# Queries of both layers and of the index: the split into two parts on whole tiles, the placing over partition halves by SBUF transfers

## The chip, the cores and the metric

The kernel runs on one core of a Trainium2 chip. The metric is the device time of one execution in microseconds (us), the median of several runs. Five engines matter: PE (TensorE, the matrix products), DVE (VectorE), ACT (ScalarE), POOL (GpSimd) and SP (SyncE, which here only issues transfers). Each engine runs its own instructions strictly in order, and waits for others by semaphores.

## The reference, cut to what matters

The model has two layers over 512 tokens of width 1024, in float32, with a squared-ReLU MLP behind each attention. What the change touches are three sets of queries:

```python
# layer A: sparse attention
q, k, v, qi, ki, wi = split(xn @ w_in)           # 16 query heads, 4 key heads, 8 index heads of 64
qi, ki = rope(qi), rope(ki)                      # index queries (8 heads) and index key (1 head)
score  = sum_h wi[t,h] * relu(qi[t,h] . ki[s])   # for blocks of 128 queries
sel    = top 128 of score among the allowed keys
o      = softmax(rope(q) . rope(k) / 8, over sel) @ v
# layer B: forgetting attention
q = xn @ w_q                                     # 16 heads of 64
o = softmax(q . k / 8 + decay, causal) @ v
```

## The kernel before, in words

**Precision.** A float32 factor is kept as two parts, hi (rounded to the fast matmul format) and lo (the rest), and a product is made of three: hi*hi, hi*lo, lo*hi. `split(hi, lo, src)` makes both: one ACT instruction writes hi, one DVE instruction writes lo = src*scale - hi.

**Two parts in one contraction.** A head has 64 features, half of the 128 partitions. The kernel uses the free half: a query tile has hi of one head on partitions 0 to 63 and lo of the same head on 64 to 127, and for the next head the halves the other way round, so that with the key's parts stacked likewise two matmuls of 128 rows do the work of three products. `unpair(dst, b, scale)` makes such a tile from a PSUM bank `b`, whose upper 64 partitions hold one head and whose lower 64 the other. In the names below `up` is partitions 0 to 63 and `dn` 64 to 127. In the kernel before it takes four instructions of 64 partitions: two on ACT for the two hi halves and two on DVE for the two lo halves. Those of lo read one half of the partitions and write the other.

**Who calls it.** `stacks` transposes a roped tile on PE (`qT<-ident,qr`, four 128x128) and calls `unpair`. `idx1` does so for the index queries `qst` of the query tiles t = 1, 2, 3 (tile 0 needs no selection), three calls; `qdone` for layer A's queries `qs`, four tiles and two halves of the heads, eight calls; `qstack` calls `unpair` directly for layer B's queries `qo`, eight calls: 19 in all.

**Who reads them.** `scores(t)` multiplies `qst` with the index key `kid` (`ix<-kid,qst`, 16 matmuls per tile); ACT takes the ReLU of each (`rl<-ix`), and DVE sums them with weights into `mask` (seven `mask<-rl,wi,mask` per tile, then one MEMSET for the keys that are not allowed). `topk(t)` then runs 16 rounds of MAX and MATCH_REPLACE over `mask` on DVE. The logits `lg<-kd,qs` and `lg<-kdup,qo` read the other two.

**Stages of layer A, by the trace.** Projections of the index (`tp<-whi,xT` and `tp<-wlo,xT` of 264 and 320 columns) to about 40 us, then keys, values and queries (512 columns), the selection and the softmax to about 188 us, the output projection after that. Layer B's queries are made at 580 to 612 us.

**What sets the order.** All instructions are first recorded and then ordered by a planner (`schedule`), which has a cost for each instruction, a latency between engines and a fixed landing time for transfers; it fills the wait of one chain with ready instructions of others. The order it finds is fixed when the program is built, and each engine runs its list. Every instruction of the program is written by the recorder's `emit`, so that all rows of the profile show its line, L423; rows are told apart by the tile names.

**Queues.** SP issues all plain transfers, in one order: weights (`raw<-in_w_...`), the inputs x and h, the output. POOL issues the transfers that add while they write (`wlo<-raw`: `wlo` holds -hi, and raw is added to it). ACT also makes the hi parts of weights (`whi<-raw`).

Of the kernel before, what the change touches and what calls it, by code (L numbers as in the profile page):

```python
# [125 lines left out]
class Recorder:  # L126
# [299 lines left out]


CFG = {
# [10 lines left out]
def body(ctx, tc, a, out):  # L439
    nc = tc.nc  # L440
    rec = Recorder(nc)
    V, S, G, PE, SP = (rec.engine(e) for e in ("DVE", "ACT", "POOL", "PE", "SP"))
# [35 lines left out]
    def scr(shape, name, dt=F32):  # L478
        return rec.tile(p_s2, shape, dt, name)

    def bank(shape, name):
        return rec.tile(p_ps, shape, F32, name, quotas.get(name))

    def small(n, name):
        return rec.tile(p_sm[n], [128, n], F32, name)
# [13 lines left out]
    def split(hi, lo, src, scale=None):  # L499
        if scale is None:  # L500
            S.copy(hi, src)
            V.tensor_tensor(lo, src, f32(hi), op=OP.subtract)
        else:
            S.activation(hi, src, AF.Copy, scale=scale)
            V.scalar_tensor_tensor(lo, src, scale, f32(hi), op0=OP.mult, op1=OP.subtract)
# [569 lines left out]
    def mlp(xT, xf, wu, wd, after, last=False):  # L1075
# [83 lines left out]
        for ci in range(4):  # L1159
# [34 lines left out]
            lastc = ci == 3  # L1194
# [2 lines left out]
                o = h[i][:, 512 * half + c.start:512 * half + c.stop]  # L1197
                add(o, src[:, c], o)

            far = CFG["dlast" if last and lastc else "dfar"]  # L1200

            def wop(y, n):
                return wop_(y, n in far)
# [88 lines left out]

    ys = {}
    mlp(xT, xf, a["w_up"][0], a["w_down"][0], afterA)

    qo = [big([128, 2, T], "qo") for _ in range(8)]
# [73 lines left out]
    e = scr([16, T], "e")  # L1370
# [62 lines left out]
    def attn(p, ks, bts):  # L1433
        pts = {}
        for e in range(2):
            q = qo[p][:, e, :]
            b0, b1, b2 = [bank([128, T], "pT") for _ in range(3)]
            rcs = small(4, "rc") if CFG["rcb"] else None
            sts = small(4, "st") if CFG["rcb"] else None
            ls = {}  # L1440
            l01 = scr([128, 384], "l")
            for t in CFG["bord"]:
                n = 128 * (t + 1)
                b = bank([128, 512], "lg")
                for i in range(2):
                    PE.matmul(b[:, :n], q[:, 128 * t:128 * t + 128], ks[e][:, i, :n], start=i == 0, stop=i == 1)
                l, mn = scr([128, n], "l") if t > 1 else l01[:, 128 * t:128 * t + n], small(1, "mn")
                st = sts[:, t:t + 1] if CFG["rcb"] else small(1, "st")
                V.tensor_tensor_reduce(out=l, in0=b[:, :n], in1=bts[e][t], op0=OP.add, op1=OP.min,
                                       scale=-1.0, scalar=BIG, accum_out=mn)  # L1450
                S.activation(l, l, AF.Exp, bias=mn, scale=-1.0, accum_out=st)
                ls[t] = l, st
            if CFG["rcb"]:
                V.reciprocal(rcs, sts)
            for t in CFG["bord"]:
                l, st = ls[t]
                if CFG["rcb"]:
                    rc = rcs[:, t:t + 1]
                else:
                    rc = small(1, "rc")  # L1460
                    V.reciprocal(rc, st)
                if CFG["bsc"] == "V":
                    V.tensor_scalar(l, l, rc, None, op0=OP.mult)
                else:
                    G.tensor_scalar(l, l, rc, 0.0, op0=OP.mult, op1=OP.add)
                PE.transpose(b0[:, 128 * t:128 * t + 128], l[:, 0:128], ident)
                if t >= 1:
                    PE.transpose(b1[:, 128 * t - 128:128 * t], l[:, 128:256], ident)
                if t >= 2:
                    PE.transpose(b2[:, 128 * t - 128:128 * t], l[:, 256:384], ident)  # L1470
                if t == 3:
                    PE.transpose(b2[:, 0:128], l[:, 384:512], ident)

            pts[e] = []
            for b in (b0, b1[:, 0:384], b2[:, 0:384]):
                if p in CFG["pvb"]:
                    pts[e].append(scr(b.shape, "pf"))
                    S.copy(pts[e][-1], b)
                else:
                    pts[e].append((scr(b.shape, "ph", F32R), scr(b.shape, "pl", F32R)))  # L1480
                    split(pts[e][-1][0], pts[e][-1][1], b)
        parts = ((0, slice(0, T), 0), (1, slice(128, T), 1), (2, slice(384, T), 3), (2, slice(256, T), 2))
        rng = lambda j: slice(0, 128) if j == 3 else slice(128, 384) if j == 2 else slice(0, T - 128 * j)
        if p in CFG["pvb"]:

            o = bank([128, T], "pv")
            for e in (1, 0):
                for x, c, j in parts:
                    PE.matmul(o[:, c] if e else o[0:64, c], vbf[j, p] if e else vbf[j, p][:, 0:64],
                              pts[e][x][:, rng(j)], start=j == 0, stop=j == 2)  # L1490
        else:
            o = oB[p // 2][:, p % 2, :] if oB else scr([128, T], "o")
            for e in range(2):

                pv, u = bank([128, T], "pv"), scr([64, T], "u")
                for x, c, j in parts:
                    for i in range(2):
                        PE.matmul(pv[:, c], vb[j][p // 4][:, (2 * p + e) % 8].flat(), pts[e][x][i][:, rng(j)],
                                  start=j + i == 0, stop=j == 2 and i == 1)
                S.copy(u, pv[64:128])  # L1500
                V.tensor_tensor(o[64 * e:64 * e + 64], pv[0:64], u, op=OP.add)
        if not oB:
            split(qo[p][:, 0, :], qo[p][:, 1, :], o)
        elif p in CFG["pvb"]:
            S.copy(oB[p // 2][:, p % 2, :], o)
# [4 lines left out]
    for p in range(8):  # L1510
        if p < 7:
            kss[p + 1] = kproj(p + 1)
        attn(p, kss[p], bts[p])
        if p < 7:
            bts[p + 1] = bias(p + 1)
# [18 lines left out]
    def afterB(t):  # L1534
# [15 lines left out]
        SP.dma_start(out[128 * t:128 * t + 128, early], hg[0])  # L1550

    mlp(xT, xf, a["w_up"][1], a["w_down"][1], afterB, last=True)

    order = rec.schedule()
# [33 lines left out]
```

## Time and profile before

| what | value |
|---|---|
| median of 3 runs | 1151.32 us (1151.09 to 1151.34) |
| profiled execution | 1147.72 us |
| its span on the core | 1145.9 us, granted clock 0.998 |
| PE busy | 1124.8 us, 98% of the span |
| DVE busy | 942.1 us, 82% |
| ACT busy | 802.5 us, 70% |
| POOL busy | 226.6 us, 20% |

The span is from the first to the last instruction; 1.8 us of the execution's time lie around it. Busy shares are means over stages with different limits, so the rows below go by stretches of time. A row that says `x16` stands for 16 instructions, with its busy time and the mean of one.

### The profile page before, as it was taken

What the parts mean: (1) busy time and instruction counts of PE and PEld (TensorE: products, weight loads), DVE (VectorE), ACT (ScalarE), POOL (GpSimd) and SP (SyncE); (2) the same over time, 40 slices, a digit from 0 to 9 for tenths busy, and PEclk for the clock granted to TensorE, in tenths of its full rate; (3) what the DMA queues carried; (4) which work ended last, traced back from release to release, by engine and by line L of the source; (5) the groups of instructions that cost most, each with busy time, mean ns of one, the idle gap of its engine ahead of it and who ended that gap; (6) DMA issues with size and microseconds to landing.
All of it is one profiled execution on the core that took longest, in us unless ns stands there. A gap on an engine that the chain in (4) does not pass through costs nothing.

```text
span 1145.9 us, 18603 instructions
## 1 busy us (share of the span) xinstructions
PE 1124.8 (98%) x6695; PEld 980.5 (86%) x6695; DVE 942.1 (82%) x1667; ACT 802.5 (70%) x1402; POOL 226.6 (20%) x378
## 2 busy tenths in 40 slices
PE   8999999999999999999999999999999999999997
PEld 8877778899899898898887878788898998998986
DVE  7999997488979979979856369764789989899687
ACT  8942899677667667569783268997676765666693
POOL 0212455100000100101110087862000100101130
PEclk9999999999999999999999999999999999999999
DMA  9871262836674674895975313597355756747892
GB/s 334 182 166 37 79 180 46 193 97 183 181 200 138 169 206 134 184 277 147 240 165 111 112 50 106 158 239 177 82 182 150 188 163 182 198 153 201 227 218 89
DMA packets 116364, 186.95 MB, mean 163 GB/s; under 512 B 8072, under 2 KB 63392, under 8 KB 116272
## 3 DMA queue, kind: packets, MB, share of 16 engines
q1 hardware_dynamic: 101008, 130.18, 34.5%
q0 software_dynamic: 15264, 55.58, 26.3%
q8 instruction: 53, 0.87, 0.3%
q14 instruction: 39, 0.32, 0.1%
HBM read 125.94 MB, written 4.23 MB: 114 GB/s over the span
## 4 chain that ended last, share of the span: by engine, by line
PE 77%; DVE 8%; issue 6%; ACT 6%; DMA 2%; POOL 1%; DVEq 0%; POOLq 0%; ACTq 0%
PE tp L423 38%; PE up L423 22%; PE qp L423 4%; PE pv L423 3%; PE lg L423 3%; PE pT L423 3%; PE kp L423 2%; DMA ulo<-raw 2%; ACT l L423 1%; DVE mask L423 1%; PE yT L423 1%; ACT whi L423 1%; ACT xT L423 1%; DVE h L423 1%; ACT kdup L423 1%
## 5 line engine op out<-in xcount | busy, mean ns | idle before, releaser
L423 PE MATMUL tp<-dhi,xhi 128*128 128x512 f32 (+1 forms) x452 | 172.1, 389 | 1.7 <-DVE h L423 1.0
L423 PE MATMUL tp<-dlo,xhi 128*128 128x512 f32 (+1 forms) x452 | 171.9, 388 | 0.0
L423 PE MATMUL tp<-dhi,xlo 128*128 128x512 f32 (+1 forms) x452 | 170.9, 388 | 0.0
L423 ACT CAST dhi<-raw 128x1024 fp32r<-128x1024 f32 x112 | 114.9, 1046 | 66.6 <-DVE raw L423 51.4
L423 PE MATMUL up<-t,uhi 128*128 128x256 f32 x896 | 148.9, 284 | 1.6 <-DVE r L423 1.6
L423 POOL DMA_DIRECT2D ulo<-raw x42 | 36.5, 870 | 516.6 <-ACT ulo L423 420.8
L423 DVE TENSOR_TENSOR dlo<-raw,dhi 128x1024 fp32r<-128x1024 f32 x100 | 121.3, 1224 | 14.9 <-ACT dhi L423 9.3
L423 PEld LDWEIGHTS up<-t,uhi 128*128 128x128 f32 x896 | 126.7, 192 | 3.3 <-DVE r L423 2.6
L423 PE MATMUL tp<-whi,xT 128*128 128x512 f32 (+2 forms) x432 | 127.6, 373 | 0.6 <-ACT xT L423 0.5
L423 PE MATMUL up<-xT,uhi 128*128 128x256 f32 x672 | 117.2, 285 | 0.2 <-DVE r L423 0.2
L423 DVE TENSOR_TENSOR raw<-raw 128x1024 f32<-128x1024 f32 x92 | 111.3, 1223 | 0.3
L423 PEld LDWEIGHTS tp<-dhi,xhi 128*128 128x128 f32 x452 | 84.9, 188 | 20.4 <-ACT xhi L423 1.1
L423 PEld LDWEIGHTS up<-xT,uhi 128*128 128x128 f32 x672 | 99.1, 191 | 2.8 <-DVE r L423 1.8
L423 PEld LDWEIGHTS tp<-dhi,xlo 128*128 128x128 f32 x452 | 84.7, 188 | 17.1
L423 PEld LDWEIGHTS tp<-dlo,xhi 128*128 128x128 f32 x452 | 84.9, 188 | 16.6
L423 PE MATMUL up<-t,ulo 128*128 128x256 f32 x448 | 96.1, 283 | 0.0
L423 PEld LDWEIGHTS tp<-whi,xT 128*128 128x128 f32 x432 | 78.2, 188 | 13.3 <-ACT xT L423 0.7
L423 ACT CAST uhi<-raw 128x1024 fp32r<-128x1024 f32 x84 | 86.0, 1044 | 4.8 <-PE up L423 4.7
L423 DVE TENSOR_TENSOR h<-tp,h 128x512 f32<-128x512 f32 (+1 forms) x97 | 65.7, 688 | 23.2 <-PE tp L423 23.1
L423 POOL TENSOR_SCALAR l<-l,rc 128x128 f32<-128x128 f32 (+3 forms) x128 | 69.6, 560 | 59.6 <-DVE rc L423 43.0
L423 PE MATMUL up<-xT,ulo 128*128 128x256 f32 x336 | 80.7, 283 | 0.0
L423 POOL DMA_DIRECT2D wlo<-raw x52 | 45.8, 902 | 176.2 <-ACT wlo L423 82.6
(213 smaller groups left out, 2717.6 us busy)
## 6 DMA issues: line engine op xcount, KB each, us to landing
raw<-in_w_down_dram SPq DMA_DIRECT2D x96, 512.0 KB, 5.3
raw<-in_w_up_dram SPq DMA_DIRECT2D x64, 512.0 KB, 5.6
wlo<-raw POOLq DMA_DIRECT2D x52, 512.0 KB, 7.1
ulo<-raw POOLq DMA_DIRECT2D x42, 512.0 KB, 5.5
raw<-in_w_kv_b_dram SPq DMA_DIRECT2D x16, 512.0 KB, 7.8
raw<-in_w_in_a_dram SPq DMA_DIRECT2D x12, 512.0 KB, 8.4
dlo<-raw POOLq DMA_DIRECT2D x12, 512.0 KB, 6.2
raw<-in_w_o_a_dram SPq DMA_DIRECT2D x8, 512.0 KB, 5.6
```

The lines of the kernel that those rows point to most:

```text
L423: getattr(self.engs[o.eng], o.fn)(*a, **k)
```

## The change

One setting changes, `CFG["swap"]` from False to True. With it, `unpair` no longer writes the halves from PSUM. It splits the whole bank, all 128 partitions at once, into two scratch tiles `nh` (hi) and `nl` (lo), with one ACT and one DVE instruction, and then has SP issue four transfers from SBUF to SBUF, of 64 partitions x 2 KB each, that place the halves:

```python
hi, lo = scr([128, 512], "nh", F32R), scr([128, 512], "nl", F32R)
split(hi, lo, b, scale=scale)
SP.dma_start(f32(d)[up, 0], f32(hi)[up])
SP.dma_start(f32(d)[dn, 0], f32(lo)[up])
SP.dma_start(f32(d)[dn, 1], f32(hi)[dn])
SP.dma_start(f32(d)[up, 1], f32(lo)[dn])
```

The diff, cut to its lines (the two new settings `dend` and `bsv` are empty, and change nothing):

```diff
 CFG = {
-    "land": 4.0, "pw": 700, "p7": (), "swap": False, "dup": False, "ufar": ("1", "2", "4"), "dfar": (), "dlast": ("1", "2", "5", "6", "3", "7"),
+    "land": 4.0, "pw": 700, "p7": (), "swap": True, "dup": False, "ufar": ("1", "2", "4"), "dfar": (), "dend": (), "bsv": (), "dlast": ("1", "2", "5", "6", "3", "7"),
...
-            far = CFG["dlast" if last and lastc else "dfar"]
+            far = CFG["dlast" if last and lastc else "dend" if lastc else "dfar"]
...
-                if CFG["bsc"] == "V":
+                if CFG["bsc"] == "V" or (p, e) in CFG["bsv"]:
```

The planner sees other instructions and finds another order. It differs in layer A's attention (up to about 235 us of the trace) and around layer B's queries; elsewhere only tile numbers differ. Three places follow, with tile names as above; a name after `<-` is what is read, and `x4` stands for four in a row.

**SP, layer A**: the loads behind the last weights of the input projection. Before:

```order
L423 DMA raw<-in_w_in_a_dram 128x2x512 x8
L423 DMA raw<-in_w_o_a_dram 128x2x512 x8
L423 DMA g<-in_g_mlp_dram 128x1024
L423 DMA raw<-in_w_up_dram 128x8x128 x4
L423 DMA h<-in_x_dram 128x1024 x4
```

and now, from the placing of the sixth `qs` on (the three of `qst` and the first five of `qs`, four transfers each, stand ahead of these rows, behind the eight loads of `w_in_a`):

```order
L423 DMA qs<-nh 64x512 x2
L423 DMA qs<-nl 64x512 x2
L423 DMA raw<-in_w_o_a_dram 128x2x512 x4
L423 DMA qs<-nh 64x512 x2
L423 DMA qs<-nl 64x512 x2
L423 DMA raw<-in_w_o_a_dram 128x2x512 x4
L423 DMA raw<-in_w_up_dram 128x8x128 x4
L423 DMA g<-in_g_mlp_dram 128x1024
L423 DMA qs<-nh 64x512 x2
L423 DMA qs<-nl 64x512 x2
L423 DMA h<-in_x_dram 128x1024 x4
```

The loads of `w_o_a` now stand behind the sixth and seventh placing of `qs`, those of `h` behind the eighth. Earlier on the same queue, three of the four `w_in_a` loads of 320 columns have moved ahead of the last two loads of x.

**PE, layer A**: the first index scores `ix` of tile 1. Before, from the last projection products ahead of them:

```order
L423 MATMUL tp<-whi,xT 128x320 x2
L423 MATMUL tp<-wlo,xT 128x320
L423 MATMUL tp<-whi,xT 128x320 x2
L423 MATMUL tp<-wlo,xT 128x320
L423 MATMUL tp<-whi,xT 128x320 x2
L423 MATMUL tp<-wlo,xT 128x320
L423 MATMUL ix<-kid,qst 128x256 x16
L423 MATMUL qT<-ident,qr 128x128 x3
L423 MATMUL tp<-whi,xT 128x320 x2
L423 MATMUL tp<-wlo,xT 128x320
```

and now:

```order
L423 MATMUL tp<-whi,xT 128x320
L423 MATMUL qT<-ident,qr 128x128
L423 MATMUL tp<-whi,xT 128x512 x6
L423 MATMUL tp<-wlo,xT 128x512
L423 MATMUL tp<-whi,xT 128x512
L423 MATMUL qT<-ident,qr 128x128 x3
L423 MATMUL tp<-whi,xT 128x512
L423 MATMUL tp<-wlo,xT 128x512
L423 MATMUL tp<-whi,xT 128x512
L423 MATMUL tp<-wlo,xT 128x512
L423 MATMUL ix<-kid,qst 128x256 x2
L423 MATMUL tp<-whi,xT 128x512 x2
```

The 16 `ix` of tile 1 stood in one piece, behind 59 products of 320 columns, 5 `qT` and none of 512 columns. Now the first stand behind 72 products of 320 columns, 12 `qT` and 12 of 512 columns, and the 16 are spread, with 20 more of 512 columns between them.

**DVE, layer A**: the lo parts of `qst` and the weighted sum of tile 1 (`mask<-rl,wi,mask` 128x256, closed by the MEMSET). Before:

```order
L423 TENSOR_TENSOR rtmp<-tp,rot 128x5x32
L423 TENSOR_TENSOR qr<-tp,rot 128x320
L423 SCALAR_TENSOR_TENSOR qst<-qT,qst 64x512 x2
L423 TENSOR_TENSOR rtmp<-tp,rot 128x5x32
L423 TENSOR_TENSOR qr<-qr,rtmp 128x320
L423 SCALAR_TENSOR_TENSOR mask<-rl,wi,mask 128x256 x6
L423 SCALAR_TENSOR_TENSOR qst<-qT,qst 64x512
L423 SCALAR_TENSOR_TENSOR mask<-rl,wi,mask 128x256
L423 SCALAR_TENSOR_TENSOR qst<-qT,qst 64x512
L423 MEMSET mask 64x64
L423 TENSOR_TENSOR rtmp<-tp,rot 128x5x32
L423 TENSOR_TENSOR qr<-tp,rot 128x320
```

and now:

```order
L423 SCALAR_TENSOR_TENSOR nl<-qT,nh 128x512
L423 TENSOR_TENSOR rtmp<-tp,rot 128x5x32
L423 TENSOR_TENSOR qr<-tp,rot 128x320
L423 TENSOR_TENSOR rtmp<-tp,rot 128x5x32
L423 TENSOR_TENSOR qr<-qr,rtmp 128x320
L423 SCALAR_TENSOR_TENSOR nl<-qT,nh 128x512
L423 SCALAR_TENSOR_TENSOR mask<-rl,wi,mask 128x256 x7
L423 MEMSET mask 64x64
L423 MAX mx<-mask 128x8
L423 MATCH_REPLACE mask<-mx,mask 128x256
L423 MAX mx<-mask 128x8
L423 MATCH_REPLACE mask<-mx,mask 128x256
```

Four half-tile `qst` stood ahead of the MEMSET, now three whole `nl`, of all three tiles (the third further up); the rope of the last tile (`rtmp`, `qr`, `rtmp`, `qr` of 320 columns) stood behind the MEMSET and now stands ahead of it.

## Rows read from the trace of the kernel before

**Rows 1.** The page's first part: busy time of each engine in us, share of the span, number of instructions.

```profile
PE 1124.8 (98%) x6695; PEld 980.5 (86%) x6695; DVE 942.1 (82%) x1667; ACT 802.5 (70%) x1402; POOL 226.6 (20%) x378
```

**Rows 2.** Busy time by stretches: layer A's attention from 42 us, its second part, the time just before it, the time after it, and a piece of its middle. Columns: start and end of the stretch, its length, then busy us and number of instructions of PE, PEld, DVE, ACT and POOL, the granted TensorE clock as a share, the busy share of the 16 DMA engines, GB/s.

```profile
42.00:188.00 146.00, 143.89 (x738) 112.84 (x738) 140.72 (x418) 102.41 (x246) 48.33 (x77) 1.00 0.43 106
110.00:188.00 78.00, 77.66 (x433) 60.08 (x432) 73.49 (x238) 70.18 (x189) 35.86 (x65) 1.00 0.38 102
30.00:42.00 12.00, 11.56 (x79) 10.79 (x78) 9.88 (x27) 11.90 (x22) 2.64 (x4) 1.00 1.06 248
188.00:235.00 47.00, 46.73 (x232) 38.20 (x231) 24.35 (x57) 35.32 (x66) 11.64 (x15) 1.00 0.63 135
90.00:120.00 30.00, 29.03 (x147) 22.49 (x146) 29.62 (x93) 10.53 (x35) 7.28 (x11) 1.00 0.11 36
```

**Rows 3.** The same for the stretch in which layer B's queries are made.

```profile
600.00:620.00 20.00, 20.00 (x90) 15.44 (x89) 10.25 (x13) 10.79 (x14) 2.62 (x3) 1.00 0.74 162
```

**Rows 4.** Two of DVE's groups by operation and shape: line, engine, operation, out<-in, shapes, number | busy us, mean ns of one | idle time ahead of them.

```profile
L423 DVE TENSOR_TENSOR pl<-pT,ph 128x512 fp32r<-128x512 f32 x42 | 27.3, 685 | 6.2 <-ACT ph L423 6.1
L423 DVE SCALAR_TENSOR_TENSOR qs<-qT,qs 64x512 fp32r<-64x512 f32 x16 | 11.0, 688 | 0.4
```

**Rows 5.** The same of ACT.

```profile
L423 ACT CAST ph<-pT 128x512 fp32r<-128x512 f32 x42 | 23.0, 593 | 0.7 <-PE pT L423 0.4
L423 ACT ACTIVATE qs<-qT 64x512 fp32r<-64x512 f32 x16 | 9.5, 592 | 27.8 <-PE qT L423 27.6
```

**Rows 6.** Instructions that write and read the tiles `qo` and `qs`: number, duration in ns (least, median, most), first and last start in us.

```profile
L423 PEld LDWEIGHTS lg<-kdup,qo x128: 186/188/208, 667.1 to 772.6; 128*128 128x128 f32 x128
L423 DVE SCALAR_TENSOR_TENSOR qo<-qp,qo x16: 683/688/694, 580.8 to 610.8; 64x512 fp32r<-64x512 f32 x16
L423 PEld LDWEIGHTS lg<-kd,qs x128: 186/189/215, 109.3 to 186.8; 128*128 128x128 f32 x128
L423 DVE SCALAR_TENSOR_TENSOR qs<-qT,qs x16: 683/688/694, 83.9 to 154.8; 64x512 fp32r<-64x512 f32 x16
```

**Rows 7.** Transfers by kind: number, KB each, median us from issue to landing; the last row is the tile view of the output tile, with the time in ns that SP takes to issue one.

```profile
raw<-in_w_in_a_dram SPq DMA_DIRECT2D x12, 512.0 KB, 8.4
raw<-in_w_o_a_dram SPq DMA_DIRECT2D x8, 512.0 KB, 5.6
h<-in_x_dram SPq DMA_DIRECT2D x4, 512.0 KB, 9.8
out_dram<-hg SPq DMA_DIRECT2D x8, 256.0 KB, 2.7
cd<-cum SPq DMA_DIRECT2D x1, 32.0 KB, 1.6
L423 SPq DMA_DIRECT2D out_dram<-hg x8: 332/382/402, 1131.3 to 1142.7; - x8
```

**Rows 8.** SP's queue in time: start, length, and the transfers issued in it.

```profile
17.55 7.76 SPq L423 DMA_DIRECT2D raw<-in_w_in_a_dram  x8
...
571.68 36.20 SPq L423 DMA_DIRECT2D raw<-in_w_kv_b_dram  x6
```

**Rows 9.** The chain of waits that ended last, between 75 and 120 us: start, length, what; the first and the last of its eight rows of `qs`.

```profile
83.93 0.68 DVE qs L423
...
104.78 0.69 DVE qs L423
```

**Rows 10.** PE in time around the first index scores: start, length from first start to last end, instruction and number. Between the first two rows stand six products of 320 columns, between the last two nine of 512 columns, nothing else in either.

```profile
34.24 0.46 PE L423 MATMUL tp<-whi,xT 128*128 128x320 f32 x2
...
35.12 2.33 PE L423 MATMUL ix<-kid,qst 128*128 128x256 f32 x16
37.29 0.49 PE L423 MATMUL qT<-ident,qr 128*128 128x128 f32 x3
37.53 0.53 PE L423 MATMUL tp<-whi,xT 128*128 128x320 f32 x2
...
47.08 0.62 PE L423 MATMUL tp<-whi,xT 128*128 128x512 f32 x2
...
49.12 0.61 PE L423 MATMUL tp<-whi,xT 128*128 128x512 f32 x2
```

**Rows 11.** DVE in time: a `qst` call, the end of the score sum of tile 1 and the first half of the rope behind it, the sixth `qs` call, and the first reader of `h`.

```profile
34.35 1.41 DVE L423 SCALAR_TENSOR_TENSOR qst<-qT,qst 64x512 fp32r<-64x512 f32 x2
...
42.53 0.11 DVE L423 MEMSET mask<- 64x64 f32 x1
42.67 0.33 DVE L423 TENSOR_TENSOR rtmp<-tp,rot 128x160 f32<-128x160 f32 x1
42.91 0.48 DVE L423 TENSOR_TENSOR qr<-tp,rot 128x320 f32<-128x320 f32 x1
...
117.51 1.39 DVE L423 SCALAR_TENSOR_TENSOR qs<-qT,qs 64x512 fp32r<-64x512 f32 x2
...
196.40 0.69 DVE L423 TENSOR_TENSOR h<-tp,h 128x512 f32<-128x512 f32 x1 [1.97 <-PE tp L423]
```

**Rows 12.** ACT in time: the first cast of `w_o_a`.

```profile
139.35 1.05 ACT L423 CAST whi<-raw 128x1024 fp32r<-128x1024 f32 x1
```

**Rows 13.** The two transfer queues over the whole span: packets, MB, and the time their packets took as a share of 16 engines' span; q1 holds the plain transfers, q0 the accumulating ones.

```profile
q1 hardware_dynamic: 101008, 130.18, 34.5%
q0 software_dynamic: 15264, 55.58, 26.3%
```

## The prediction

> **What bounds the kernel now.** I read the page's busy line first [rows 1]. PE reads 98% busy, which tempts one to price the change on PE alone; but it adds and removes no matmul, so what counts is where PE waits for the engines that do change. The busy time by stretch [rows 2] shows it. Over layer A's attention, 42 to 188 us, DVE works 140.72 of 146 us: only 5.28 us idle. From 188 to 235 us the picture turns: PE 46.73 of 47, DVE 24.35. So DVE sets the pace with PE until about 188 us, and PE alone after that. Where layer B's queries are made [rows 3] PE is busy 20.00 of 20, with DVE at 10.25 and ACT at 10.79.
>
> What the change touches costs DVE 688 ns and ACT 592 ns for each half of a tile [rows 4, 5]. The rows that settle what the change saves are the neighbours with all 128 partitions: `pl<-pT,ph` 128x512 takes 685 ns on DVE, `ph<-pT` 128x512 takes 593 ns on ACT. Half the partitions cost as much time as all of them.
>
> **The change, part by part.** There are 19 calls: 3 for `qst`, 8 for `qs`, 8 for `qo`. Each had two ACT and two DVE instructions and now has one of each, so ACT loses 19 x 0.592 = 11.2 us and DVE 19 x 0.688 = 13.1 us. Each call gains four transfers of 64 partitions x 2 KB, 76 in all, 9.7 MB, and with them one hop between the split and the matmul.
>
> *Layer B (8 calls): 0.* ACT and DVE lose 4.7 and 5.5 us where PE is the bound [rows 3], so nothing is gained. The hop is covered: DVE writes `qo` from 580.8 to 610.8 us, and its first reader on PE starts at 667.1 [rows 6], over 50 us later. SP issues 32 transfers more, 0.38 us each by the issue time of `out_dram<-hg` [rows 7], 12 us, in a stretch where six `w_kv_b` loads were spread over 36.20 us [rows 8]. If that cover were gone, a load would be late by at most those 12 us; nothing in the trace shows it that tight. I take 0, and no more than 1 us either way.
>
> *Layer A, what DVE saves: -5.5 us of its work.* Eleven calls remove 7.6 us. The three of `qst` come while DVE still waits for PE and ACT, so I count only the eight of `qs` here: 8 x 0.688 = 5.5 us, all inside the saturated stretch. The chain of waits has these very instructions on it, eight between 83.93 and 105.5 us [rows 9].
>
> *Layer A, what the extra hop costs: the index scores come later.* The planner knows the transfer and fills PE with other products first. Before, the first `ix` stood at 35.12 us [rows 10]. Ahead of it now stand 13 more `tp` of 320 columns, 7 more `qT` and 12 `tp` of 512 columns. Their price by the starts in the timeline: six of 320 in 35.12 - 34.24 = 0.88, so 0.147 each; three `qT` in 0.24, 0.08 each; nine of 512 in 49.12 - 47.08 = 2.04, 0.227 each. 13 x 0.147 + 7 x 0.08 + 12 x 0.227 = 5.2, so the first `ix` comes at 40.3. Among the 16 `ix` of this tile stand 20 more of 512 columns: 20 x 0.227 + 16 x 0.136 (2.17 us for 16) = 6.7, so the last ends at 47.0. PE loses nothing, these products are only made earlier. DVE does: the sum of the scores, whose end shows as the MEMSET at 42.53 [rows 11], would end some 1.3 us after the last `ix`, at 48.3: one `rl` on ACT and two scaled sums on DVE are left, of 256 columns, each shorter than the 0.59 and 0.69 us of 512 columns [rows 4, 5]. ACT is full here (11.90 of 12 us, [rows 2]), and a pair of its casts in the way, 2 x 1.05 us [rows 12], gives 50.3 as the other end. DVE's lag at that point is 5.8 to 7.8 us. Set against it is work done meanwhile that stood later: one rope of twice 0.33 and twice 0.48, 1.6 us [rows 11], and the `qst` of the last tile, two of 0.688, 1.4 us. The lag is 2.8 to 4.8 us.
>
> *Sum for DVE in layer A:* 2.8 to 4.8 less 5.5 gives -2.7 to -0.7; I take the middle, -1.7.
>
> *What passes to the end.* DVE shares the pace with PE: from 110 to 188 us PE is busy 77.66 of 78 and DVE 73.49 [rows 2]. A DVE microsecond won there moves PE only where PE was waiting for DVE's softmax work. I take somewhat over half: -1.0 us. Bounds are none and all.
>
> *Queues.* The eight `w_o_a` loads now stand behind the sixth and seventh `qs` placing, the `h` loads behind the eighth. SP stands at a transfer until its split is done, so all of them wait with it. The sixth split ended at 117.51 + 1.39 = 118.9 us before [rows 11]; the first cast of `w_o_a` is at 139.35 [rows 12], and a load takes 5.6 us to land [rows 7]: 15 us to spare. The eighth ended at 154.8 + 0.7 = 155.5 [rows 6]; `h` takes 9.8 to land [rows 7], 165.3, and is first read at 196.40 [rows 11]. Both are covered, 0. The last two loads of x move behind three weight loads of 7.76 / 8 = 0.97 us each [rows 8], 2.9 us; PE now has the 320-column products of those weights to do meanwhile: 0, with 2.9 us as the bound if it had none. POOL's queue is not moved past.
>
> *The transfers themselves.* No row before shows an SBUF-to-SBUF transfer. From below, the quickest landing is `cd<-cum`, 1.6 us; `out_dram<-hg`, twice as large, takes 2.7 us; from above 512 KB loads take 8.4 us [rows 7]. With the DMA engines nearly idle (0.11 of 90 to 120 us, [rows 2]) I take 2.7 plus 4 x 0.38 of issue, 4.2 us, for `qs`. The first `qs` was split at 83.9 + 1.4 = 85.3 us and read at 109.3 [rows 6], so it is covered. For `qst` the DMA engines are full, and that is rival C.
>
> Sum: 1147.72 - 1.0 + 0 = 1146.7 us for the profiled execution, which ran 3.6 us under the median of the runs, 1151.32. So **1150.3 us**. 0.2%, 2.3 us, is about what a measurement of this kernel can tell from no change.
>
> **Rivals.** *B, faster by about 4 us.* DVE's idle gap is filled with ropes and maxima of other tiles, so the lag vanishes and the saving counts nearly whole: 0 to 1.5 lag against 5.5 gives -4.0 (1147.3), and -7.6 if all eleven calls pass. For it: the `qs` rows lie on the chain [rows 9]. Against: the order of DVE has no maxima before the late score sum, and PE's share is full.
>
> *C, slower by about 3 us: PE stands at the first `ix`.* PE runs in order, so if `qst` lands after 40.3 us, everything behind `ix` waits. The split of the first tile ended at 34.35 + 1.41 = 35.8 us before [rows 11]; by the order its four `qT` now have 3.7 us less of PE's products ahead, so 32. SP issued the last load of the stretch before at 25.3 us (17.55 + 7.76, [rows 8]); it lands some 8.4 us later, 33.7. From 30 to 42 us the DMA share is 1.06 [rows 2]: all 16 engines full, with accumulating transfers of `wlo` among them. A packet of the plain queue took 0.345 x 16 x 1145.9 / 101008 = 63 ns, one of the accumulating queue 0.263 x 16 x 1145.9 / 15264 = 316 ns [rows 13]. The four transfers are 256 packets, 16 to an engine: 1.0 us alone, 16 x 0.379 = 6.1 us if each waits for one accumulating packet. From 33.7 plus 6.1 and the issue of four: 40 to 41.5 us. That is at PE's arrival, 40.3. The point from which it decides is a landing after about 42; at 44.5 PE loses 4 us, which the stages behind cannot give back since PE is full. Net +3: 1154.3. Against it: the plan has put 5 us of cover there, and the casts hold back the accumulating transfers.
>
> The Trainium skill ("DMA: Bandwidth & Descriptors", Queues, rings and completion order) says that a DMA engine takes the queue rows that have work in turn, a packet at a time. By that rule the alternating price of C holds, not the lone one; a row of before can't show it, since nothing small was timed in a full stretch. By it the first `qst` lands at 40 to 41.5 us, by the lone price at about 36; the time would be 1154.3 at the far end of the one and 1150.3 by the other.
>
> *D, the change doesn't save what it says,* because the halves come back elsewhere: the order of DVE shows one `nl` per call and no other addition, so this is out.
>
> **How the numbers follow.** The forecast case, 1148.0 to 1153.0, has 0.42; B, about 1144 to 1148.5, has 0.31; C, 1153.5 to 1158, has 0.27. The likeliest is 1150.3. The range 1145.5 to 1155.5 leaves out the far end of B (-7.6) and of C, about 0.1 each. Faster by over 0.2% (below 1149.0): B and a sixth of the forecast case, 0.37. Slower (above 1153.6): C less its near end, 0.25. Between: 0.38.
>
> **What the profile after would show.** Right: DVE one `nl` of about 0.69 us per call, 11 of them before 160 us; the first `ix` near 40.3 with no wait over 1 us; the MEMSET between 48 and 50.5; DVE's idle time between 42 and 188 not far from 5.28 us; layer B's length unchanged. Wrong by B: the first `h<-tp,h` near 192.5 us with the score sum on time. Wrong by C: PE idle before `ix`, released by a DMA from `nh` or `nl`, and a landing over 8 us. Layer B's readers of `qo` waiting for a DMA, or a `raw` of `w_kv_b` late, would refute the 0 there.

## The result, and the profile after

The change made the kernel slower: 1165.91 us median (1160.11 to 1166.14, 5 runs) against 1151.32, a ratio of 1.0125 [1.0102, 1.0148], 14.4 us. The forecast, 1150.3 us in a range to 1155.5, was wrong, and the place was the one that rival C names. One execution of e18 below, at 1835 us with a granted clock of 0.556, is left out of its row.

The profiled execution took 1165.2 us with a span of 1163.4, 17.5 us more than before. Layer B's first query product starts at 572.4 us, before at 554.6: 17.8 us later. So all of the loss is made ahead of layer B's queries. First the same stretches as [rows 2] (the fourth is moved by 17 us with the program):

```profile
30.00:42.00 12.00, 10.97 (x72) 9.85 (x70) 7.49 (x27) 12.00 (x17) 5.19 (x6) 1.00 1.07 264
42.00:188.00 146.00, 131.95 (x665) 103.84 (x666) 119.33 (x374) 80.60 (x208) 39.62 (x65) 0.95 0.55 141
110.00:188.00 78.00, 72.96 (x394) 56.39 (x393) 66.82 (x230) 53.28 (x153) 30.10 (x56) 0.98 0.60 169
205.00:252.00 47.00, 46.65 (x231) 37.08 (x229) 23.84 (x53) 34.75 (x63) 11.92 (x16) 1.00 0.64 135
```

DVE's idle time between 42 and 188 us has grown from 5.28 to 26.67 us, and PE's from 2.1 to 14.05. The clock's mean in this stretch is 0.95. The waits of PE between 20 and 240 us say where (engine, what was waited for, us in total, times, longest):

```profile
PE ix L423 <- DMA qst<-nl: 9.8, 1, 9.8
PE lg L423 <- DVE mn L423: 3.6, 1, 3.6
PE pv L423 <- ACT pf L423: 1.4, 1, 1.4
```

**The first wait.** PE in time, columns as in [rows 10], with the idle time and its releaser in brackets:

```profile
40.58 0.40 PE L423 MATMUL tp<-wlo,xT 128*128 128x512 f32 x1
50.80 0.77 PE L423 MATMUL ix<-kid,qst 128*128 128x256 f32 x2 [9.82 <-DMA qst<-nl]
51.37 1.06 PE L423 MATMUL tp<-whi,xT 128*128 128x512 f32 x2
52.22 0.63 PE L423 MATMUL tp<-wlo,xT 128*128 128x512 f32 x1
...
54.57 0.40 PE L423 MATMUL tp<-whi,xT 128*128 128x512 f32 x1
54.80 0.39 PE L423 MATMUL tp<-wlo,xT 128*128 128x512 f32 x1
```

PE came to the first `ix` at 50.80 - 9.82 = 40.98 us (forecast: 40.3) and stood until the transfers of `qst` had landed. What follows is slow as well: two products of 512 columns from 51.37 take 0.85 us, at 54.57 one takes 0.23. The granted clock shows why:

```profile
50.80:54.30 3.50, 3.50 (x10) 2.98 (x11) 0.00 (x0) 1.86 (x4) 0.00 (x0) 0.50 1.08 241
54.30:60.00 5.70, 5.70 (x32) 4.90 (x31) 3.13 (x7) 5.20 (x11) 0.00 (x0) 1.00 0.49 120
172.00:175.00 3.00, 2.76 (x10) 2.19 (x11) 3.00 (x10) 0.00 (x0) 0.74 (x2) 0.79 0.99 359
175.00:177.30 2.30, 2.30 (x9) 1.78 (x8) 0.89 (x4) 1.90 (x5) 2.30 (x5) 0.53 0.94 374
...
289.80:293.20 3.40, 3.40 (x19) 3.40 (x18) 2.12 (x3) 1.64 (x2) 0.00 (x0) 0.50 0.00 0
```

It is 0.50, the level of 1.2 GHz, for the 3.5 us behind PE's standstill, and 1.00 again from 54.3 on: half of 3.5 us is lost once more, 1.75 us. The same happens behind the second wait (below), some 3.4 us at 0.50 between 172 and 177.3 (3.0 x 0.21 / 0.5 + 2.3 x 0.47 / 0.5), 1.7 us lost. A third such stretch, from 289.8 to 293.2 us, costs another 1.7 us; it stands behind a wait of 2.2 us for DVE. In before that wait is 1.3 us, in e13 (below) 2.5 us, and the clock stays at 1.00 in both, so this third stretch is not shown to come of the change.

DVE, columns as in [rows 11]:

```profile
41.19 0.69 DVE L423 SCALAR_TENSOR_TENSOR nl<-qT,nh 128x512 fp32r<-128x512 f32 x1 [1.90 <-ACT nh L423]
54.58 1.09 DVE L423 SCALAR_TENSOR_TENSOR mask<-rl,wi,mask 128x256 f32<-128x256 f32 x2 [12.70 <-ACT rl L423]
...
60.33 0.11 DVE L423 MEMSET mask<- 64x64 f32 x1
...
128.18 0.29 DVE L423 CUSTOM_DVE_ANT_0 l<-lg,mask 128x128 f32<-128x128 f32 x1 [2.49 <-DMA qs<-nh]
...
171.62 0.56 DVE L423 CUSTOM_DVE_ANT_0 l<-lg,mask 128x384 f32<-128x384 f32 x1 [3.81 <-DMA qs<-nh]
```

The score sum ends at 60.33, forecast 48.3 to 50.3, with 12.70 us of waiting in one piece ahead of it. And there is a **second wait**, at 171.62: `l<-lg,mask` reads no `qs`, and yet a transfer of `qs<-nh` released it; PE's 3.6 us at `lg` follow from it. A shorter wait of the same kind stands at 128.18, behind the sixth placing of `qs`, and reaches PE as the 1.4 us at `pv`.

The transfers that place `qst`, as SP issues them (tile view: number, issue time in ns, first and last start; then us from issue to landing, least, median, most), and the two queues between 40 and 45 us (packets, MB, share of 16 engines):

```profile
L423 SPq DMA_DIRECT2D qst<-nh x6: 461/495/599, 29.2 to 48.8; - x6
L423 SPq DMA_DIRECT2D qst<-nl x6: 461/502/663, 30.4 to 52.4; - x6
...
DMA to landing us min/median/max: 6.8/17.6/21.4
```

```profile
q0 software_dynamic: 234, 0.83, 83.6%
q1 hardware_dynamic: 226, 0.37, 23.5%
```

They took 17.6 us in the median, up to 21.4, where those of `qs`, most of them in a nearly empty stretch, took 2.5. While both queues have work, each gets about as many packets as the other (234 and 226), but the accumulating ones take 84% of the engines' time: the plain queue moves 0.37 MB in 5 us. From 25 to 30 us, with no accumulating packet, it moved five times as much:

```profile
q1 hardware_dynamic: 1000, 1.93, 105.2%
```

The Trainium skill ("DMA: Bandwidth & Descriptors", Queues, rings and completion order) says that an engine takes the rows with work in turn, a packet at a time; the trace agrees, with 234 packets against 226.

The instructions themselves came out as forecast, whole tiles at the price of the halves in [rows 4, 5]:

```profile
L423 DVE SCALAR_TENSOR_TENSOR nl<-qT,nh 128x512 fp32r<-128x512 f32 x11 | 7.4, 677 | 2.4 <-ACT nh L423 2.3
L423 ACT ACTIVATE nh<-qT 128x512 fp32r<-128x512 f32 x11 | 6.7, 608 | 25.9 <-PE qT L423 21.4 <-DVE mask L423 4.4
```

### The profile page after: what moved, and what is told of

It is laid out like the page before. It is cut to its first block, busy times and chain, and to the rows that moved or that the text cites. A ratio compares the mean times of both kernels' runs of the same rounds, so it can differ in the third digit from the quotient of the medians.

```text
span 1163.4 us, 18742 instructions
## 1 busy us (share of the span) xinstructions
PE 1129.0 (97%) x6695; PEld 984.0 (85%) x6695; DVE 927.8 (80%) x1648; ACT 790.2 (68%) x1383; POOL 226.4 (19%) x378
## 4 chain that ended last, share of the span: by engine, by line
PE 66%; DVE 5%; ACT 3%; DMA 1%; issue 1%; POOL 0%; DVEq 0%; ACTq 0%
PE tp L423 31%; PE up L423 25%; PE qp L423 4%; PE kp L423 2%; PE pT L423 1%; PE pv L423 1%; PE lg L423 1%; DMA ulo<-raw 1%; ACT l L423 1%; DVE h L423 1%; PE yT L423 1%; ACT kdup L423 1%; DVE xlo L423 1%; DVE kdup L423 1%; DVE raw L423 0%
## 5 line engine op out<-in xcount | busy, mean ns | idle before, releaser
L423 PEld LDWEIGHTS tp<-whi,xT 128*128 128x128 f32 x432 | 78.5, 190 | 13.2 <-ACT xT L423 0.9
```

The costliest lines, as they stand in the source:

```text
L423: getattr(self.engs[o.eng], o.fn)(*a, **k)
```

## The experiments

The theory from these rows: two waits for transfers, each with the low clock behind it, make the loss. The first is `qst` in a queue that has loads ahead and shares the engines with accumulating transfers; the second is a slot, a piece of on-chip memory that several scratch tiles use in turn, since `nh` and `nl` stay occupied until their transfers have read them. The rivals: the later index scores cost by themselves; the loads ahead alone are to blame. All runs, with the kernel before on the same chip in each:

| run | median us (range, runs) | before | ratio [95%] | us |
|---|---|---|---|---|
| change | 1165.9 (1160.1 to 1166.1, 5) | 1151.3 | 1.0125 [1.0102, 1.0148] | +14.4 |
| e15 change again | 1161.6 (1158.1 to 1164.6, 4) | 1148.7 | 1.0121 [1.0097, 1.0146] | +13.9 |
| e2 qst undone | 1149.0 (1146.9 to 1150.5, 10) | 1147.6 | 1.0007 [0.9996, 1.0018] | +0.8 |
| e3 qst alone | 1160.7 (1156.4 to 1166.5, 4) | 1147.6 | 1.0113 [1.0075, 1.0152] | +13.0 |
| e4 qo alone | 1148.8 (1146.7 to 1151.2, 10) | 1147.6 | 1.0008 [0.9997, 1.0019] | +0.9 |
| e1 qst on ACT's queue | 1167.0 (1166.1 to 1167.3, 4) | 1147.6 | 1.0163 [1.0145, 1.0181] | +18.7 |
| e12 short accumulating transfers | 1153.0 (1150.1 to 1155.2, 9) | 1149.5 | 1.0030 [1.0018, 1.0041] | +3.4 |
| e9 no wait for qst | 1152.1 (1150.5 to 1154.9, 10) | 1149.5 | 1.0029 [1.0016, 1.0042] | +3.3 |
| e10 loads behind qs | 1157.9 (1149.0 to 1163.4, 9) | 1149.5 | 1.0070 [1.0044, 1.0095] | +8.0 |
| e18 e9 and e10 | 1151.2 (1147.1 to 1155.1, 11) | 1149.8 | 1.0010 [0.9994, 1.0026] | +1.1 |
| e13 neither wait | 1145.4 (1144.4 to 1152.4, 9) | 1148.7 | 0.9978 [0.9962, 0.9994] | -2.5 |
| e14 planned late | 1161.1 (1160.9 to 1166.6, 4) | 1148.7 | 1.0124 [1.0103, 1.0144] | +14.2 |
| e11 qs alone, loads behind | 1148.3 (1145.7 to 1152.7, 12) | 1149.5 | 0.9996 [0.9982, 1.0010] | -0.5 |
| e5 no accumulating transfers | 1145.8 (1144.7 to 1149.1, 10) | 1148.7 | 0.9985 [0.9974, 0.9996] | -1.7 |
| e17 before, so set | 1156.6 (1153.3 to 1159.8, 6) | 1149.8 | 1.0060 [1.0041, 1.0079] | +6.9 |
| e16 e5, loads behind qs | 1147.4 (1145.0 to 1149.1, 11) | 1149.8 | 0.9977 [0.9965, 0.9989] | -2.6 |

The last column is the ratio less one, times before. In e9, e12, e13 and e18 a part of the result is not computed, as said at each, so that they show times alone.

**Which of the three sets of queries.** `unpair` got a tag, and the new way holds for the tags of a list:

```diff
-        if CFG["swap"]:
+        if tag in CFG["swap"]:      # e2: ("qs", "qo"); e3: ("qst",); e4: ("qo",)
```

> qst as before (halves written by ACT and DVE), qs and qo as in the change; the planner finds its order anew. Theory: the 9.8 us of PE's wait and the 3 us of low clock behind it go, the ix stand at 35 us again; what stays is the wait near 170 us, PE 3.6 us and a low clock behind it, less what DVE saves: 1150 to 1155 us. Rival (the wait near 170 us and its own order are worth as much as the one at 41 us): 1156 to 1160 us.

> Only qst placed by transfers, qs and qo as before. Theory: the wait at the first ix is all there, about 10 us and 3 us of low clock, and the wait near 170 us is gone: 1162 to 1166 us. Rival (the two halves of the change share the loss about equally): 1156 to 1160 us.

> Only layer B's qo placed by transfers. Theory (PE is the bound there, and the readers come 50 us later): 1150.3 to 1152.3 us, no PE wait for a transfer. Rival (32 transfers ahead of the w_kv_b loads on SP make those late): 2 us or more slower, 1153.5 or above, with PE or ACT waiting for raw of w_kv_b.

With `qst` undone the loss is gone; with `qst` alone it is 13.0 of 14.4 us. Layer B costs nothing that can be told from 0 (+0.9, [-0.3, +2.2]). The second wait, which e2 was expected to keep, costs PE little in e2's own order: DVE still waits 3.3 and 1.5 us at `l` for transfers, but PE stands 0.3 and 1.4 us behind them and the clock stays at 1.00. The runs of e3 spread over 10 us, from 1156.4 to 1166.5: in its profile, the fastest of them, the landing took 13.2 us at most and PE stood 1.7 us at `ix`, in the change's 21.4 and 9.8.

The landing of `qst` differs from profile to profile, and PE's wait with it: 10.2 us in the median and 1.7 us of waiting in e3, 14.2 and 5.8 in e15, 17.6 and 9.8 in the change, 20.3 and 12.4 in e10. What goes with it is the time of the issue. Where the granted clock is 1.00 over the first 30 us (change, e9, e10, e13, e14), the first transfer is issued at 28.2 to 29.2 us and the landing takes 14.8 to 20.3 us; where it is 0.94 (e3, e15, e18), PE makes the index queries later, the issue comes at 30.3 to 30.5 us and the landing takes 10.2 to 14.2 us. That the later issue finds fewer loads ahead of it is likely; no run tests it.

**Why it landed late.** In e1 every order stays, only the engine that issues changes; in e12 the accumulating transfers stay in number and order, but move a sixteenth:

```diff
-            getattr(self.engs[o.eng], o.fn)(*a, **k)
+            getattr(self.nc.scalar if <transfer into qst> else self.engs[o.eng], o.fn)(*a, **k)   # e1
+            # e12: first 8 of POOL: lo[:, :, 0:32], raw[:, :, 0:32]
```

> The changed kernel with every engine's order kept; only the twelve transfers that place qst are issued by ACT, so they enter a queue of their own and not SP's queue behind the eight loads of w_in_a. Theory (they stood behind those loads in SP's queue, and that queue got every other packet from the accumulating transfers): the first four land within 5 to 9 us of their issue in place of 17 to 21, PE waits 0 to 2 us at the first ix in place of 9.8, the clock stays up, and 10 to 13 us come back: 1153 to 1156 us. Rival (only the sharing with the accumulating transfers matters, whatever the queue): they still land after 45 us and PE waits 5 us or more: 1160 to 1166 us.

> The changed kernel in its own order, but each of the first eight accumulating transfers wlo<-raw moves 32 columns of each row of 512 only (the low part of these weights is wrong by that). Theory (loads ahead in SP's queue and the accumulating transfers share the DMA engines packet by packet, and it is the sharing that makes the queue slow): qst lands within 8 us of its issue, PE waits at the first ix 0 to 2 us, and the time comes to that of the run without PE's wait, 1 to 9 us slower than before. Rival (the eight loads ahead in the queue alone): it still takes 15 us or more, PE waits over 6 us, 12 us or more slower than before.

e12 settles it. The transfers of `qst` land in 3.1 us, with the same loads ahead of them, in place of 17.6 (or of 10.2 to 14.2 where, as in e12, the issue comes after 30 us):

```profile
DMA to landing us min/median/max: 2.3/3.1/6.5
```

PE's wait is gone, and the time is that of e9, where the wait is taken out at its other end. So it is the accumulating transfers' traffic that makes the queue slow. e1 did not give the time back, against what was expected, and taught something else: from a queue of its own the landing fell to 7.3 us in the median, with the first issue at 30.6 us. Issues as late on SP's queue took 10.2 to 14.2 us, so the loads ahead are only a part of the landing. And ACT, in order, now stood at the issues while its casts and `mask<-ix` waited behind them. ACT's waits from 20 to 60 us, and PE's:

```profile
ACT whi L423 <- issue: 5.3, 1, 5.3
ACT mask L423 <- issue: 3.6, 1, 3.6
```

```profile
PE ix L423 <- DVE nl L423: 5.1, 1, 5.1
PE ix L423 <- ACT mask L423: 3.0, 1, 3.0
```

**What the waits cost, and what the order costs without them.** In the order of the change, `ix` reads `kid` (e9), and with that the sixth and eighth `qs` are filled from `kd`, so that their transfers hold neither `nh` nor `nl` (e13). The index scores, and in e13 those queries, are not computed by that:

```diff
+    if o.fn == "matmul" and "ix" in n:
+        return [a[0], real(kid[:, 0, 0:128]), a[2]]          # e9, e13, e18
+    if <transfer into the sixth or eighth qs>:
+        return [a[0], real(kd[p:p + 64, 0])]                 # e13
```

> The changed kernel in its own order, but the index scores ix multiply kid with kid in place of qst (so this part of the result is not computed); all transfers still run, and PE no longer waits for those of qst. Against the kernel before of the same job, where the change was 14 to 19 us slower. Theory (the wait for the transfer and the low clock behind it are the loss, 13 us): 1 to 4 us slower than before. Rival (the later place of the index scores in the order costs DVE much by itself, as the 8 us slower profile of the run with qst alone hints, where PE waited only 1.7 us): 6 to 9 us slower, DVE idle over 8 us between 30 and 60 us.

> The changed kernel in its own order with both waits for transfers taken out: the index scores multiply kid with kid in place of qst, and the transfers of the sixth and eighth qs read kd in place of nh and nl, so that no slot is held by them (both parts of the result are not computed rightly by that). Theory (the order as such costs nothing, as the forecast had it; all of the change's loss is the wait for qst, the slot that the last transfers of qs hold, and the low clock behind each): within 2 us of before, 3 us or more better than the run that took out the first wait alone (3.3 us slower than before). Rival (the later scores cost DVE 3 us by themselves): still 3 us slower than before.

Without the first wait 3.3 us are left, without both -2.5 us [-4.4, -0.7]. The stretch from 150 to 180 us, of e9 and of e13:

```profile
150.00:180.00 30.00, 25.99 (x139) 20.61 (x139) 22.69 (x63) 23.82 (x61) 12.74 (x21) 0.94 0.48 138
```

```profile
150.00:180.00 30.00, 30.00 (x165) 24.16 (x164) 28.14 (x78) 29.44 (x73) 14.49 (x24) 1.00 0.55 148
```

With the slots free PE is busy 30.00 of 30 and the clock stays at 1.00. The order itself, with the score sum at 48.7 us where the order puts it, is not slower but 2.5 us faster: the rival that blamed it fell. That says nothing of a sum that ends at 60.33 us, as in the change; e14 below has one.

**The second wait's loads.** On SP, `w_up` and `g` go behind the eighth placing (e10), the same with `ix` free (e18):

```diff
-        for o in order:
+        for o in reorder(order):    # SP's loads that stood between the transfers of qs: after the last of them
```

> The changed kernel in its own order, but on SP the four loads of w_up and that of g stand behind the eighth placing of qs and not ahead of it. Theory (near 171 us DVE waits for a slot that the transfers of the eighth qs still read, because 13 loads are ahead of them): the last transfers land within 3.5 us, DVE's wait of 3.8 us and PE's of 3.6 us go and the clock stays up: 4 to 6 us of the change's loss come back, 9 to 13 us slower than before. Rival (another wait takes its place): as slow as the change, 14 us or more.

> The changed kernel in its own order, with the first wait taken out (index scores multiply kid with kid, so this part is not computed) and on SP the loads of w_up and g behind the eighth placing of qs. Theory (the second wait comes of loads ahead of the last transfers): of the 3.3 us that the run without the first wait was slower than before, 2 us or more go: 2 us faster to 1.5 us slower than before. Rival (the loads of w_o_a and the accumulating transfers are enough to hold the slot): 2 to 3.5 us slower, DVE still waits over 2 us.

e10 can't be read in its time: its runs cover 14 us, since the first wait is in it (12.4 us in its profile). In the profiles DVE's wait at `l` falls from 3.8 to 2.4 us in e10, and from 4.2 to 2.4 in e18. e18 is 1.1 us slower than before [-0.7, +3.0], e9 was 3.3 [1.8, 4.8]: the intervals overlap, so that the moved loads hold about half of the wait is likely and not shown.

**Covering the wait by planning.** The planner was told that a transfer into `qst` lands 14 us later:

```diff
-                    o.end = dma[0] + (CFG["land"] if e != "POOL" else 3.5)
+                    o.end = dma[0] + (CFG["land"] if e != "POOL" else 3.5) + 14.0 * <transfer into qst>
```

> The whole change, but the planner is told that a transfer into qst lands 14 us later than it assumed, and puts 74 products of 512 columns ahead of the first ix in place of 12. Theory (DVE paces this stage, so work that reaches it 14 us later costs as much as PE standing; only the low clock is saved): 8 to 14 us slower than before, no PE wait at ix. Rival (PE is the pace, and a wait covered by other products is free): 3 to 6 us slower, as in the run where ix didn't wait.

PE no longer stands at `ix`, it is busy 30.00 of 30 us with the clock at 1.00, and nothing is gained (+14.2). DVE waits instead, 14.5 us in one piece, for the first score, whose sum ends at 60.22 us:

```profile
30.00:60.00 30.00, 30.00 (x162) 25.95 (x161) 10.77 (x33) 22.53 (x36) 9.19 (x11) 1.00 1.07 247
```

```profile
DVE mask L423 <- ACT mask L423: 14.5, 1, 14.5
DVE l L423 <- DMA qs<-nh: 6.6, 1, 6.6
```

PE then stands later, 6.2 us at `lg` and 2.8 us at `pT`, and the clock's mean from 42 to 188 us is 0.96. The slot wait is longer here too (6.6 us), so not all of the 14.2 is the late scores'.

**What is left of the idea.** e11 has the new way for `qs` alone, and SP's order as in e10; e5 and e17 change one setting, the list of weights whose low parts accumulating transfers make, in whose place DVE makes those of `w_in_a` (e5 in the change, e17 in the kernel before), and e16 is e5 with SP's order as in e10; e15 is the change as it is:

```diff
-    "swap": True,
+    "swap": ("qs",),                      # e11
-    "dl": ("a", "oa", "up0", "up1", "q", "v", "ob"),
+    "dl": ("oa", "up0", "up1", "q", "v", "ob"),   # e5, e17, e16
```

> Only qs placed by transfers, qst and qo as before, the order planned for that, and on SP the loads of g and w_up behind the eighth placing. Theory (DVE's saving of 8 x 0.67 us passes to the end where nothing waits for a transfer): 2 to 4 us faster than before. Rival (PE is the bound in the second half of the stage, or slots held by the transfers eat it): within 1.5 us of before.

> The whole change, but the low parts of the weights of layer A's keys, values and queries made by DVE and not by accumulating transfers, the order planned for that. Theory (without the accumulating transfers the placing of qst is quick): qst lands within 10 us, PE waits under 2 us for it; DVE has 8 x 1.22 = 9.8 us more to do, part of it ahead of 42 us: 2 to 8 us slower than before, better than the change. Rival (loads alone fill the queue): PE still waits over 5 us, 12 us or more slower.

> The kernel before with the low parts of layer A's key, value and query weights made by DVE, nothing else. Theory (the change itself brings the gain of 1 to 2 us once its transfers are not slowed; the setting alone costs DVE up to 9.8 us): the same as before or up to 5 us slower. Rival (the setting alone is the gain): 1 to 3 us faster than before.

> The whole change with the low parts made by DVE, and on SP the loads of w_up and g behind the eighth placing of qs. Theory (the last slot wait, 1.2 us on DVE there, goes): 2 to 4 us faster than before. Rival (PE paces that part): as the run without the move, 1 to 2 us faster.

> The changed kernel itself, on the chip of these three, to compare with. Between 11 and 19 us slower than before, with the two waits in the trace; its runs spread over several us, since the landing of qst varies.

`qs` alone, without a wait, gains nothing that can be told (-0.5, [-2.1, +1.1]), where 2 to 4 us were expected. Between 120 and 150 us DVE then idles and PE does not:

```profile
120.00:150.00 30.00, 29.68 (x165) 22.45 (x163) 22.73 (x81) 24.38 (x63) 12.90 (x24) 1.00 0.62 182
```

In e5 one setting differs (`"dl"` loses `"a"`): DVE makes the low parts of the eight weights, and no accumulating transfer runs while `qst` is placed. `qst` lands in 2.3 us median, and the whole change is 1.7 us faster than before [-3.0, -0.5], where 2 to 8 us slower was expected. It is not the setting alone that brings it: the kernel before with this setting is 6.9 us slower. Each of the two runs has an order of its own from the planner. With the loads behind the eighth placing as well (e16) it is 2.6 us faster [-4.0, -1.3]: a version that beats both kernels, though the step from e5 to e16 is within their intervals.

## Why the prediction was wrong

- **"For `qst` the DMA engines are full, and that is rival C"** is the step that failed: the sum that gave 1150.3 us has PE's wait at the first `ix` at 0, and C, which has it, has it too small. C had the place, the mechanism (PE in order at the first `ix`, behind loads and accumulating transfers) and its own mark of proof; but it let the first `qst` land at 40 to 41.5 us, and PE lose 4 us at the far end. It landed at 50.8, PE lost 9.8, and the low clock 1.75 more. The price of a packet pair was right: 0.379 us, against 5 us x 16 / 226 = 0.354 us measured. The backlog was too small. I let the last load land at 33.7 us; the plain queue of the change from 32 us, just behind the start of the sharing, to 44 us, to 50.8 us and to 60 us (queue, packets, MB, share):

```profile
q1 hardware_dynamic: 547, 0.96, 24.3%
```

```profile
q1 hardware_dynamic: 794, 1.36, 22.2%
```

```profile
q1 hardware_dynamic: 1163, 1.95, 21.3%
```

  Of the 1.95 MB the twelve transfers of `qst` are 1.57 (12 x 64 x 2 KB), so some 0.38 MB of loads were still ahead at 32 us, and at the shared rate (0.96 MB in 12 us) they alone take 4.8 us, the four transfers with 0.52 MB another 6.5: 43.3 us in all. That is 2 us past my bound. They landed later still, 18 us and more after issues from 29.2 us on, and PE was released at 50.8. Where these further 7 us are is open: by then the queue had moved 1.36 MB, 0.46 more than the 0.90 of the loads and the first four, so that packets of the next placings had passed while a last one of the first was missing. The sum is a mean over 16 engines, a transfer lands with its last packet, and no view here gives the engine of a packet. That they hang on the accumulating transfers is shown by e12; that their size varies, by e3 and e15 (PE waited 1.7 and 5.8 us). That the 9.8 us are lost by PE's standstill itself is not shown: in e14 PE is kept busy there and the loss stays, so late scores cost by way of DVE as well, and how the loss divides between the two is open.
- **"Both are covered, 0" and "it is covered"** missed a reader. I asked when `qs`, `w_o_a` and `h` are read, and those were covered indeed: no row of the change shows PE waiting for them. I didn't ask when `nh` and `nl` come free. Their slots pass to `l`, and the transfers hold them: 3.6 us of PE and 1.7 us of clock behind the eighth placing, 1.4 us of PE behind the sixth.
- **The low clock** behind a standstill of PE was in no term; in the profile it is 1.75, 1.7 and 1.7 us.
- **The sum without the waits** was right in sign: the order alone, e13, is 2.5 us faster, forecast 1.0, with bounds from -0.7 to -2.7 us for DVE. Near to that, 2.7 us, is what PE lost in before to short waits between 20 and 240 us (for `qr`, `kr` and `qst` above all), of which the change has 0.4 left. The score sum without the wait ends at 48.49 us in e9, forecast 48.3.
- Together, for PE in the profile: 9.8 + 1.75 + 3.6 + 1.7 = 16.9 us for the two waits, with 1.4 at `pv` and 1.7 for the third stretch of low clock 20.0, less the 2.5 of e13, is 17.5 us, the difference of the two profiles' spans. The 14.4 us are the difference of the medians, and before's median lay 3.6 us over its profile. That the sum closes to a tenth is luck: e13's gain has an interval of 3.7 us and is from another chip.
- **Layer B** was right: forecast 0, no more than 1 us either way, measured +0.9 [-0.3, +2.2].
- **"I take somewhat over half"** of DVE's saving stays open for the parts: e11 shows PE taking over where DVE saves, yet e13 gains 2.5 us.

## What to carry to other kernels

A transfer that replaces an engine's copy must be priced by the traffic of the moment at which it is issued: the same 128 KB took 2.5 us in a quiet stretch and 17.6 among accumulating transfers, and an in-order engine behind it stood 9.8 us, with 3.5 us at half the clock after that. Ask of its source as well as of its target: the buffer stays occupied until the transfer has read it, and whoever takes the slot next waits. Filling the wait with other work of the waiting engine doesn't help where another engine, fed by the late result, sets the pace (e14).

## What the runs showed that was not expected

An issue can be dear for the engine that issues. In e1 those of `qst<-nl` between 38 and 60 us took ACT 1.5 to 2.5 us each; on SP, which computes nothing, they took 0.46 to 0.66 us in the change and up to 1.96 us in e3, where the landings were shorter (10.2 us median): it looks as if part of the wait had only moved from the queue to the issuer, which no run tests. And the time of one kernel can spread by 10 us: e3's four runs go from 1156.4 to 1166.5 us where those of before on the same chip stay between 1146.3 and 1150.1.
